# Down projection of a decoder layer: the residual put into three PSUM banks by ScalarE, four merged sums, and the last gated chunk turned, fetched and split at other places in the order

## The chip, the core and the metric

The kernel runs on one core of one Trainium2 chip. The metric is the device time of one execution in microseconds (us); lower is better. TensorE (PE, with its weight loads PEld), VectorE (DVE), ScalarE (ACT), GpSimd (POOL) and SyncE (SP, which here only issues DMAs) each run their own list of instructions in order and wait for each other by semaphores.

## The reference, cut to what matters

One decoder layer over 256 tokens of width 1024, all in float32: a mixer, a cross-attention, and a SwiGLU feed-forward block, each followed by a residual sum and a layer norm. The change is in the last block:

```
h2  = layer_norm(ALPHA * h1 + cross_attention, ln2)          # 256 x 1024
g   = silu(h2 @ w_gate) * (h2 @ w_up)                        # 256 x 2816
out = layer_norm(ALPHA * h2 + g @ w_down, ln3)               # 256 x 1024
```

ALPHA is the fourth root of 2. The last line is what the changed code computes: the product with `w_down`, the residual `ALPHA * h2`, and the sum of the two.

## The kernel before, in words

**Products.** Every float32 operand is split into a high and a low part that TensorE can multiply exactly enough: ScalarE rounds the operand to `hi`, VectorE subtracts it (`lo = x - hi`), and each product is three matmuls (hi by hi, lo by hi, hi by lo; function `three`, L351 to L353). Weight rows come from HBM by SP's DMAs into raw buffers (`w133r`), and the splits of one weight row are one ScalarE copy (`w133h`, L144 or L157) and one VectorE subtraction (`w133l`, L145 or L158), both 128x1024. There are nine buffers for split weights and seven for raw ones.

**Gate and up.** The 2816 columns are eleven chunks of 256 (`NFC = 11`, c = 0 to 10). For each chunk, `proj_n` makes two PSUM banks `pg` (one per 128 tokens, t = 0 and 1), then `gated(c, t, ...)` takes the silu on ScalarE (L942) and the product on VectorE (L943) into `sg`.

**Turning a chunk.** For the down product, g must lie with its columns on the partitions. `gated_out(c)` transposes `sg` in 32x32 blocks on VectorE (`gs<-sg`, L435) and sends it to DRAM by one DMA on SP's queue (`gd<-gs`, L438). `gated_in(c)` reads it back by four DMAs on SP's queue (`gr<-gd`, L446). `gated_split(c)` splits it: `gTh` on ScalarE (L414), `gTl` on VectorE (L415).

**Down.** The output of 256x1024 is four quadrants: C11, C12 (tokens 0 to 127, left and right half), C21, C22 (tokens 128 to 255), each one PSUM bank; in the code they are `acc[PIECES[0]]` to `acc[PIECES[3]]`. For the first nine chunks (`SEVEN = 9`) the products use Strassen's scheme with seven products for eight, where four of them (p1, p5, p6, p7) are gathered in banks of their own (`shared`, made during the gate-and-up loop by `shared_products`), and the others go straight into C11, C12 and C21. The merge is C11 += p1, C12 += p1+p6+p5, C21 += p1+p6+p7, C22 += p1+p6+p7+p5. The last two chunks (four weight rows, w135 to w138) are multiplied in the plain way, quadrant after quadrant, in the tail of `down()`; C22 is made there in two pieces of 256 columns, the second in a bank of its own (`own`).

**The order around the change.** All engines run in the order in which the code issues. `down()` is a generator that yields after each product; a loop of 23 steps (step 0 to 22) runs it, and a table `events` says what is issued ahead of which step. One product is 3 matmuls. Steps 0 to 22 cover all products of the first nine chunks except four that go into C21 later; behind step 22 come the seeds (below) and the plain products of C11, C12, C21 and the two pieces of C22. The function `get` also issues the splits of weight rows, nine rows ahead, so these lie between the events on ScalarE and VectorE.

**Merge and residual before.** `merge()` runs in eight parts at steps 8, 9, 11, 13, 14, 16, 17 and 19: it copies p1 to SBUF on ScalarE (`u1`, L1103), and makes on VectorE, in eight instructions of 128x512, the sums u2 and u3 and, for each quadrant, `r = ALPHA * h2 + sum` (L1100, and L1110, L1119 for p5). The four `r` are then added to the banks ("seeds", L1068): for C12 and C21 behind step 22, for C22's two pieces behind C11's statistics, and for C11 in the sum L1174. C22's bank gets its first two matmuls (L1157) ahead of C21's products, so that there is something to add to.

**The end.** Per 128 tokens: statistics (`bn_stats`, L715, two to four of them), their aggregate (L722), a power on POOL (L724), and two passes on VectorE per half (L729 or L1182, then L735), then the stores. The last piece of tokens 128 to 255 ends on TensorE and ScalarE (L1209 to L1217).

Of the kernel before, what the change touches and what calls it, by code (L numbers as in the profile page):

```python
# [11 lines left out]
OP = mybir.AluOpType  # L12
AX = mybir.AxisListType

P = 128
D = 1024
S = 256
T = S // P
# [6 lines left out]
NFC = DFF // CW  # L25
WINDOWS = (2, 4, 8, 16)
PADW = 16
ALPHA = 2.0 ** 0.25
# [7 lines left out]
SEVEN, LAG, LATE = 9, 2, 4  # L36
# [6 lines left out]
class Stream:  # L43
# [118 lines left out]
    def next(self):  # L162

        i = len(self.tiles)
        return i + (2 if i < len(self.items) and self.items[i][0] == "sums" else 1)
# [6 lines left out]
    def get(self, numbers, k):  # L172

        n = self.count(numbers[0])
        self.prepare(numbers[k // n] + 1, True)
        self.asked += 1
        if not self.held and self.asked % self.pace == 0:
            self.prepare(min(self.used + AHEAD, self.next()))
        hi, lo = self.tiles[numbers[k // n]]
        return hi[:, k % n, :], lo[:, k % n, :]  # L180
# [13 lines left out]
def decoder_layer(  # L194
# [3 lines left out]
    nc = tc.nc  # L198
# [17 lines left out]
    def accbank(name):  # L216
        return pa.tile([P, 512], F32, tag="acc", name=name)


    ws = Stream(nc, wp)  # L220
# [42 lines left out]
    for c in range(NFC):  # L263
        c_gu.append(ws.add(w_gu[c], 4))
        n = c - LAG
# [89 lines left out]
    def pair(hl, *ix):  # L355
        return hl[0][ix], hl[1][ix]

    ALL = slice(None)
# [46 lines left out]
    def run(gen, n=None):  # L405

        while n is None or n > 0:
            if next(gen, gen) is gen:
                return False
            n = None if n is None else n - 1  # L410
        return True

    def split(h, l, ps):
        nc.scalar.copy(h, ps)  # L414
        nc.vector.tensor_sub(l, ps, r32(h))  # L415
# [227 lines left out]
    v, u, xk = do_v(), do_u(), do_xk()  # L643
# [102 lines left out]
    PIECES = tuple((t, *half) for t in range(T) for half in HALVES)  # L746
# [49 lines left out]
    for t in range(T):  # L796
        norm = Norm(1, xt[:, t, :], h1[:, t, :])
# [105 lines left out]
    h2 = ap.tile([P, T, D], F32, tag="a8", name="h2")  # L903
# [17 lines left out]
    norm = Norm(2, h1[:, 0, :], h2[:, 0, :])  # L921
# [3 lines left out]
    norm = Norm(2, h1[:, 1, :], h2[:, 1, :])  # L925
# [13 lines left out]
    def gated(c, t, ps):  # L939

        sg = sgs[c][:, :, t, :]
        nc.scalar.activation(sg, ps[:, :CW].rearrange("p (f b) -> p f b", f=2), AF.Silu, bias=0.0, scale=1.0)  # L942
        nc.vector.tensor_mul(sg, sg, ps[:, CW:].rearrange("p (f b) -> p f b", f=2))  # L943
# [3 lines left out]
    def gated_out(c):  # L947
        via[c] = turned([(0, sgs[c].rearrange("p f t b -> p (f t) b"))], 4, "g")

    def gated_in(c):  # L950
        via[c] = landed(via[c], 4, "g")
# [25 lines left out]
    def fourth_split(c0, c1):  # L977
        hl = [sp.tile([P, 4, P], F32R, name=f"S4{n}", tag="pr", bufs=PR_BUFS) for n in range(2)]
        for c in range(c0, c1):
            s4[c] = hl[0][:, c - c0], hl[1][:, c - c0]  # L980
        split(*[s[:, :c1 - c0] for s in hl], s_raw["fourth"][:, c0:c1])

    def gated_split(c):
        i, f = divmod(2 * c, KD)
        h, l = [g[:, f:f + 2, :].rearrange("p f (t i b) -> p (f t) i b", t=T, i=4) for g in gT[i]]
        split(h, l, via[c].rearrange("p i m b -> p m i b"))

    begun = set()
# [37 lines left out]
    def by_row():  # L1026

        for gen in gu1:
            while run(gen, 2):
                yield  # L1030

    for c in range(1, NFC):
        sgs.append(sp.tile([P, 2, T, P], F32, name="sg", tag="pr", bufs=PR_BUFS))
        pss = {t: second[t] if c == 1 else accbank("pg") for t in range(T)}
        gu = by_row() if c == 1 else proj_n(pss, c_gu[c], h2T)
        run(gu, 1)
        gated_out(c - 1)
        run(gu, 2)
        if c > 1:
            gated_split(c - 2)  # L1040
            if c - 2 < SEVEN:
                token_sums(c - 2)
        run(gu, 2)
        gated_in(c - 1)
        run(gu, 1)
        if 0 <= c - 2 < SEVEN:
            token_sums_split(c - 2)
        if c == NFC - 1:
            fourth_split(0, 4)
        run(gu)  # L1050
        for t in range(T):
            gated(c, t, pss[t])
        if 0 <= c - LAG < SEVEN:
            shared_products(c - LAG)

# [3 lines left out]

    LAST = 768  # L1060
    norms = []
    acc = {PIECES[n]: accbank("acc") for n in (2, 0, 1, 3)}
    C11, C12, C21, C22 = [acc[piece] for piece in PIECES]
    acc[1, 512, LAST] = C22[:, :LAST - 512]

    def seed(t, c0, c1, ps):

        nc.vector.tensor_add(ps, norms[t].r[:, c0:c1], ps)  # L1068

    def four(c0, c1):  # L1070

# [16 lines left out]
    def merge():  # L1088

        p1, p5, p6, p7 = shared  # L1090
        for t in range(T):
            norms.append(Norm(3, h2[:, t, :]))
        r = [norms[t].r[:, h * 512:(h + 1) * 512] for t in range(T) for h in range(2)]
        tok = [h2[:, t, h * 512:(h + 1) * 512] for t in range(T) for h in range(2)]

        def u(i):
            return sp.tile([P, 512], F32, name=f"u{i}", tag="pr", bufs=PR_BUFS)

        def onto(n, u):
            nc.vector.scalar_tensor_tensor(r[n], tok[n], ALPHA, u, op0=OP.mult, op1=OP.add)  # L1100

        u1, u2 = u(1), u(2)
        nc.scalar.copy(u1, p1)  # L1103
        nc.vector.tensor_add(u2, u1, p6)
        yield
        onto(0, u1)
        yield
        onto(1, u2)
        yield
        nc.vector.tensor_add(r[1], r[1], p5)  # L1110
        yield
        u3 = u(3)
        nc.vector.tensor_add(u3, u2, p7)
        yield
        onto(2, u3)
        yield
        onto(3, u3)
        yield
        nc.vector.tensor_add(r[3], r[3], p5)  # L1119
        yield  # L1120

    def down():

        yield from fourth(SEVEN - 1, SEVEN)
        yield from four(SEVEN - 1, SEVEN)
        for c in range(0, SEVEN - 1, 2):
            if c < LATE:
                yield from fourth(c, c + 2)
            yield from four(c, c + 2)
        load_norm("g", 3, ln3_g)()  # L1130
        load_norm("b", 3, ln3_b)()
        get = lambda k: (gT[k // KD][0][:, k % KD], gT[k // KD][1][:, k % KD])
        rest = [c_dn[c][f] for c in range(SEVEN, NFC) for f in range(2)]
        done = 2 * SEVEN
        acc[1, LAST, D] = bank("acc")[:, :D - LAST]
        ws.prepare(ws.used + AHEAD)
        ws.held = True
        seed(*PIECES[1], acc[PIECES[1]])
        seed(*PIECES[2], acc[PIECES[2]])
        for piece in (*PIECES[:3], (1, 512, LAST), (1, LAST, D)):  # L1140
            t, c0, c1 = piece
            if piece == PIECES[2]:
                for c in range(LATE, SEVEN - 1, 2):
                    yield from fourth(c, c + 2)
            for j, numbers in enumerate(rest):
                y_hi, y_lo = pair(get(done + j), ALL, slice(t * P, (t + 1) * P))
                hi, lo = [w[:, c0:c1] for w in ws.get(numbers, 0)]
                end = j == len(rest) - 1
                if j or (t, c0) not in ((1, 512), (1, LAST)):
                    nc.tensor.matmul(acc[piece], y_hi, hi, start=False, stop=False, skip_group_check=True)  # L1150
                nc.tensor.matmul(acc[piece], y_hi, lo, start=False, stop=False, skip_group_check=True)
                nc.tensor.matmul(acc[piece], y_lo, hi, start=False, stop=end, skip_group_check=True)
                yield
            if piece == PIECES[1]:
                y_hi = pair(get(done), ALL, slice(P, 2 * P))[0]
                for c0, c1 in ((512, LAST), (LAST, D)):
                    nc.tensor.matmul(acc[1, c0, c1], y_hi, ws.get(rest[0], 0)[0][:, c0:c1], start=True, stop=False,  # L1157
                                     skip_group_check=True)
            yield piece

    dn, parts = down(), merge()
    events = {
        2: lambda: gated_out(NFC - 1), 4: lambda: fourth_split(4, SEVEN - 1), 6: lambda: gated_split(NFC - 2),
        7: lambda: gated_in(NFC - 1), 18: lambda: gated_split(NFC - 1),
    }
    events.update({step: lambda: run(parts, 1) for step in (8, 9, 11, 13, 14, 16, 17, 19)})
    for step in range(23):
        events.get(step, lambda: None)()
        run(dn, 1)
# [1 line left out]
    until(dn)  # L1171
    norm = norms[0]
    for c in (0, 256):
        nc.vector.tensor_add(norm.r[:, c:c + 256], norm.r[:, c:c + 256], acc[PIECES[0]][:, c:c + 256])  # L1174
        norm.measure(c, c + 256)

    def measure(norm, ps):
        for c in range(0, ps.shape[1], 256):
# [5 lines left out]

    until(dn)
    own = acc[1, LAST, D]
    seed(1, 512, LAST, acc[1, 512, LAST])
    seed(1, LAST, D, own)
    measure(norm, acc[PIECES[1]])
    norm.stats()  # L1190
    norm.centre(0, 512)
# [8 lines left out]
    norm = norms[1]  # L1200
# [67 lines left out]
```

## Time and profile before

| | |
|---|---|
| median of 3 runs | 371.18 us (371.0 to 372.96) |
| the profiled execution | 370.71 us; its span from first to last instruction 368.9 us |
| TensorE busy | 360.5 us, 98% of the span, 1995 matmuls |
| VectorE busy | 312.1 us, 85% |
| ScalarE busy | 197.3 us, 53% |
| POOL busy | 68.9 us, 19% |
| granted TensorE clock | 0.996 |
| HBM traffic | 241 GB/s over the span |

The profile is of one execution. All times on the timeline are microseconds from the span's start. A row of the timeline is: start, duration, engine, line, operation, output<-inputs, shape, count, and in brackets how long the engine had been idle and what released it. The duration of an instruction is longer than its distance to the next one where two overlap in the engine's pipeline: TensorE's 128x512 matmuls have 0.39 us each and start 0.23 us apart. The line numbers L are those of the kernel before, unless the text says otherwise.

### The profile page before, as it was taken

What the parts mean: (1) busy time and instruction counts of PE and PEld (TensorE: products, weight loads), DVE (VectorE), ACT (ScalarE), POOL (GpSimd) and SP (SyncE); (2) the same over time, 40 slices, a digit from 0 to 9 for tenths busy, and PEclk for the clock granted to TensorE, in tenths of its full rate; (3) what the DMA queues carried; (4) which work ended last, traced back from release to release, by engine and by line L of the source; (5) the groups of instructions that cost most, each with busy time, mean ns of one, the idle gap of its engine ahead of it and who ended that gap; (6) DMA issues with size and microseconds to landing.
All of it is one profiled execution on the core that took longest, in us unless ns stands there. A gap on an engine that the chain in (4) does not pass through costs nothing.

```text
span 368.9 us, 5709 instructions
## 1 busy us (share of the span) xinstructions
PE 360.5 (98%) x1995; PEld 311.3 (84%) x1995; DVE 312.1 (85%) x462; ACT 197.3 (53%) x298; POOL 68.9 (19%) x102
## 2 busy tenths in 40 slices
PE   9999999999999999999999999999999999999893
PEld 9997998997888899988888888888888888888682
DVE  5778899994699788765879989999998999789974
ACT  5666865753153665564127636754764664579101
POOL 1000058140010003220010024315402422400000
PEclk9999999999999999999999999999999999999998
DMA  7997699699525995944105988779769877656311
GB/s 246 416 421 297 207 318 327 247 253 396 211 89 167 370 372 203 329 148 151 57 2 198 344 287 285 289 245 346 266 224 338 274 270 262 225 170 195 117 49 65
DMA packets 33836, 89.24 MB, mean 242 GB/s; under 512 B 4240, under 2 KB 12304, under 8 KB 33680
## 3 DMA queue, kind: packets, MB, share of 16 engines
q1 hardware_dynamic: 31520, 83.77, 64.0%
q0 software_dynamic: 1712, 4.72, 4.0%
q10 hardware_dynamic: 576, 0.39, 0.3%
q8 instruction: 15, 0.25, 0.3%
q14 instruction: 13, 0.11, 0.1%
HBM read 81.53 MB, written 7.34 MB: 241 GB/s over the span
## 4 chain that ended last, share of the span: by engine, by line
PE 93%; DVE 4%; issue 1%; ACT 0%; DVEq 0%
PE pg L352 11%; PE pg L351 11%; PE pg L353 11%; PE pxk L369 6%; PE pxq L369 6%; PE pqk L487 6%; PE acc L351 4%; PE acc L352 4%; PE acc L353 4%; PE pu L369 3%; PE x L352 2%; PE x L351 2%; PE x L353 2%; PE xv L352 2%; PE xv L351 2%; PE xv L353 2%
## 5 line engine op out<-in xcount | busy, mean ns | idle before, releaser
L962 POOL TENSOR_TENSOR sraw<-gr 128x128 f32<-128x128 f32 x9 | 9.8, 1094 | 94.7 <-DMA gr<-gd 87.8
L724 POOL TENSOR_TENSOR rs<-mv,mhalf 128x1 f32<-128x1 f32 x6 | 4.4, 735 | 100.2 <-DVE mv L722 100.2
L438 POOL DMA_DIRECT2D pd<-ps x4 | 2.4, 612 | 48.4 <-DVE ps L435 48.1
L524 ACT ACTIVATE pr<-pr,mx 128x128 f32<-128x128 f32 (+1 forms) x16 | 7.1, 444 | 8.2 <-DVE mx L555 8.2
L963 POOL TENSOR_TENSOR sraw<-sraw,gr 128x128 f32<-128x128 f32 x9 | 10.7, 1192 | 0.7
L1204 ACT COPY r<-acc 128x512 f32<-128x512 f32 (+1 forms) x2 | 1.0, 480 | 17.2 <-DVE st L715 17.1
L414 ACT CAST h2Th<-tp 128x512 fp32r<-128x512 f32 x4 | 2.4, 588 | 14.6 <-PE tp L425 14.6
L446 POOL DMA_DIRECT2D pt<-pd x16 | 8.8, 555 | 6.6 <-ACT w23h L144 3.7
L942 ACT ACTIVATE sg<-pg 128x256 f32<-128x256 f32 x22 | 7.9, 381 | 3.2 <-PE pg L353 3.1
L964 POOL TENSOR_TENSOR sraw<-gr 128x128 f32<-128x128 f32 x9 | 9.1, 1009 | 0.0
L943 DVE TENSOR_TENSOR sg<-sg,pg 128x256 f32<-128x256 f32 x22 | 8.4, 415 | 0.4 <-ACT sg L942 0.3
L446 POOL DMA_DIRECT2D xr<-xd x12 | 6.6, 560 | 8.5 <-DMA xd<-xs 5.3
L414 ACT CAST gTh<-gr 128x512 fp32r<-128x512 f32 x11 | 6.8, 614 | 2.6 <-DMA gr<-gd 2.6
L415 DVE TENSOR_TENSOR gTl<-gr,gTh 128x512 fp32r<-128x512 f32 x11 | 7.8, 708 | 0.4 <-ACT gTh L414 0.4
L438 POOL DMA_DIRECT2D xd<-xs x3 | 1.7, 576 | 34.0 <-DVE xs L435 34.0
L435 DVE STREAM_TRANSPOSE gs<-sg 128x512 f32<-128x512 f32 x11 | 7.7, 701 | 0.0
L729 DVE SCALAR_TENSOR_TENSOR r<-r,mv,g 128x512 f32<-128x512 f32 (+1 forms) x10 | 7.5, 781 | 0.2
L524 ACT ACTIVATE xpr<-xs,mx 128x256 f32<-128x256 f32 x8 | 3.7, 470 | 7.0 <-DVE mx L535 7.0
L414 ACT CAST S<-sraw 128x384 fp32r<-128x384 f32 (+1 forms) x9 | 4.7, 523 | 4.6 <-POOL sraw L964 4.6
L715 DVE BATCH_NORM_STATS2 st<-r 128x6 f32<-128x512 f32 (+1 forms) x10 | 6.4, 641 | 0.3
L529 DVE RECIPROCAL sm<-sm 128x2 f32<-128x2 f32 x12 | 2.0, 164 | 5.5 <-ACT xpr L524 4.4
L531 DVE TENSOR_SCALAR pr<-pr,sm 128x128 f32<-128x128 f32 (+1 forms) x16 | 6.1, 422 | 0.3
(1389 smaller groups left out, 1501.0 us busy)
## 6 DMA issues: line engine op xcount, KB each, us to landing
gd<-gs SPq DMA_DIRECT2D x11, 256.0 KB, 5.5
gr<-gd SPq DMA_DIRECT2D x44, 64.0 KB, 2.0
pd<-ps POOLq DMA_DIRECT2D x4, 384.0 KB, 4.2
pt<-pd POOLq DMA_DIRECT2D x16, 96.0 KB, 7.3
g<-in_ln_g SPq DMA_DIRECT2D x3, 512.0 KB, 4.4
b<-in_ln_b SPq DMA_DIRECT2D x3, 512.0 KB, 6.1
wr<-in_w_qkv SPq DMA_DIRECT2D x5, 256.0 KB, 4.8
mr<-in_mem_t SPq DMA_DIRECT2D x1, 1024.0 KB, 12.0
```

The lines of the kernel that those rows point to most:

```text
L351: nc.tensor.matmul(ps, wa, ya, start=start, stop=False, skip_group_check=part)
L352: nc.tensor.matmul(ps, wa, yb, start=False, stop=False, skip_group_check=part)
L353: nc.tensor.matmul(ps, wb, ya, start=False, stop=stop, skip_group_check=part)
L369: nc.tensor.matmul(pss[f], w[:, s], y, start=k == 0 and f == 0 and n == 0, stop=k == KD - 1 and n == 2, skip_group_check=True)
L414: nc.scalar.copy(h, ps)
L446: queue.dma_start(raw[32 * j:32 * (j + 1)].rearrange("p i m b -> p i (m b)"), via[:, j, :].rearrange("(i a) r -> a i r", i=4))
L487: nc.tensor.matmul(qk[i][:, f, :], w[:, c * P:(c + 1) * P], y, start=k == 0 and f == 0 and w is hi and y is x_hi, stop=k == KD - 1 and w i ...
L524: nc.scalar.activation(dst[:, j, :], src[:, j, :], AF.Exp, bias=mx[:, j:j + 1], scale=sign, accum_out=sm[:, j:j + 1])
L943: nc.vector.tensor_mul(sg, sg, ps[:, CW:].rearrange("p (f b) -> p f b", f=2))
L962: nc.gpsimd.tensor_add(s1, a21, a22)
L963: nc.gpsimd.tensor_sub(s2, s1, a11)
L964: nc.gpsimd.tensor_sub(s3, a11, a21)
```

## The change

It does five things.

1. The residual goes into PSUM first. A new function `residual(n)` takes quadrant n's bank and writes `ALPHA * h2` into it by one ScalarE instruction (128x512). It is called for C21 and C11 in the last round of the gate-and-up loop, ahead of that round's remaining products, and for C12 behind `gated` of the last chunk. The banks are noted as begun, so that the products add to what is there.
2. `merge()` makes four sums without the residual (p1; p1+p6+p5; p1+p6+p7; that + p5) in one ScalarE copy and four VectorE adds, of which the first makes p1+p6 for the other three: at steps 8, 16 and 17, and the last one (C22's) behind C11's sum and statistics.
3. The seeds of C12 and C21 add `merged[n]`; C11's sum reads `merged[0]`; C22's two pieces are now written by VectorE (`ALPHA * h2 + merged[3]`, L1182 of the changed kernel) ahead of all their products.
4. C22's two early matmuls go back to the head of their own pieces, so all products there add.
5. The last chunk: `gated_out(10)` moves from step 2 to directly behind `gated` of that chunk, `gated_in(10)` from step 7 to step 5, `gated_split(10)` from step 18 to step 12.

```diff
+    acc = {}
+
+    def residual(n):
+
+        t, c0, c1 = PIECES[n]
+        acc[PIECES[n]] = accbank("acc")
+        begun.add(id(acc[PIECES[n]]))
+        nc.scalar.mul(acc[PIECES[n]], h2[:, t, c0:c1], ALPHA)
...
             fourth_split(0, 4)
+            residual(2)
+            residual(0)
         run(gu)
         for t in range(T):
             gated(c, t, pss[t])
+        if c == NFC - 1:
+            gated_out(c)
+            residual(1)
         if 0 <= c - LAG < SEVEN:
             shared_products(c - LAG)
...
-    acc = {PIECES[n]: accbank("acc") for n in (2, 0, 1, 3)}
+    acc[PIECES[3]] = accbank("acc")
+    merged = {}
...
-        u1, u2 = u(1), u(2)
-        nc.scalar.copy(u1, p1)
-        nc.vector.tensor_add(u2, u1, p6)
+        merged.update({n: u(n) for n in (0, 4)})
+        nc.scalar.copy(merged[0], p1)
+        nc.vector.tensor_add(merged[4], merged[0], p6)
         yield
-        onto(0, u1)
+        merged[1] = u(1)
+        nc.vector.tensor_add(merged[1], merged[4], p5)
         yield
-        onto(1, u2)
+        merged[2] = u(2)
+        nc.vector.tensor_add(merged[2], merged[4], p7)
         yield
-        nc.vector.tensor_add(r[1], r[1], p5)
-        yield
-        u3 = u(3)
-        nc.vector.tensor_add(u3, u2, p7)
-        yield
-        onto(2, u3)
-        yield
-        onto(3, u3)
-        yield
-        nc.vector.tensor_add(r[3], r[3], p5)
-        yield
+        merged[3] = u(3)
+        nc.vector.tensor_add(merged[3], merged[2], p5)
...
-        seed(*PIECES[1], acc[PIECES[1]])
-        seed(*PIECES[2], acc[PIECES[2]])
+        for n in (1, 2):
+            nc.vector.tensor_add(acc[PIECES[n]], merged[n], acc[PIECES[n]])
...
-            if piece == PIECES[1]:
-                y_hi = pair(get(done), ALL, slice(P, 2 * P))[0]
-                for c0, c1 in ((512, LAST), (LAST, D)):
-                    nc.tensor.matmul(acc[1, c0, c1], y_hi, ws.get(rest[0], 0)[0][:, c0:c1], start=True, stop=False,
-                                     skip_group_check=True)
...
-        2: lambda: gated_out(NFC - 1), 4: lambda: fourth_split(4, SEVEN - 1), 6: lambda: gated_split(NFC - 2),
-        7: lambda: gated_in(NFC - 1), 18: lambda: gated_split(NFC - 1),
+        4: lambda: fourth_split(4, SEVEN - 1), 5: lambda: gated_in(NFC - 1), 6: lambda: gated_split(NFC - 2),
+        12: lambda: gated_split(NFC - 1),
     }
-    events.update({step: lambda: run(parts, 1) for step in (8, 9, 11, 13, 14, 16, 17, 19)})
+    events.update({step: lambda: run(parts, 1) for step in (8, 16, 17)})
...
-        nc.vector.tensor_add(norm.r[:, c:c + 256], norm.r[:, c:c + 256], acc[PIECES[0]][:, c:c + 256])
+        nc.vector.tensor_add(norm.r[:, c:c + 256], merged[0][:, c:c + 256], acc[PIECES[0]][:, c:c + 256])
         norm.measure(c, c + 256)
+    run(parts)
...
-    seed(1, 512, LAST, acc[1, 512, LAST])
-    seed(1, LAST, D, own)
+    for c0, c1 in ((512, LAST), (LAST, D)):
+        nc.vector.scalar_tensor_tensor(acc[1, c0, c1], h2[:, 1, c0:c1], ALPHA, merged[3][:, c0 - 512:c1 - 512],
+                                       op0=OP.mult, op1=OP.add)
```

The first place is VectorE in the second half of the 23 steps, from the split of w134 to the seeds of C12 and C21. `u` are the merged sums, `x` the banks of p5 to p7, `h` is h2, `r` the residual sums, `gTl` is here the last chunk's low part. Before:

```order
L158 TENSOR_TENSOR w134l<-t_3106,w134h 128x1024
L1100 SCALAR_TENSOR_TENSOR r<-h_1881,u_3604 128x512
L145 TENSOR_TENSOR w135l<-w130r,w135h 128x1024
L1110 TENSOR_TENSOR r<-r,x 128x512
L145 TENSOR_TENSOR w136l<-w131r,w136h 128x1024
L1113 TENSOR_TENSOR u_3640<-u_3604,x 128x512
L145 TENSOR_TENSOR w137l<-w132r,w137h 128x1024
L1100 SCALAR_TENSOR_TENSOR r<-h_1881,u_3640 128x512 x2
L145 TENSOR_TENSOR w138l<-w133r,w138h 128x1024
L415 TENSOR_TENSOR gTl_2066<-gr,gTh_2065 128x512
L1119 TENSOR_TENSOR r<-r,x 128x512
L1068 TENSOR_TENSOR acc<-r,acc 128x512 x2
```

And the same stretch of VectorE's list after the change (with the changed kernel's line numbers):

```order
L158 TENSOR_TENSOR w134l<-t_3106,w134h 128x1024
L145 TENSOR_TENSOR w135l<-w130r,w135h 128x1024
L415 TENSOR_TENSOR gTl_2066<-gr,gTh_2065 128x512
L145 TENSOR_TENSOR w136l<-w131r,w136h 128x1024
L145 TENSOR_TENSOR w137l<-w132r,w137h 128x1024
L1113 TENSOR_TENSOR u_3652<-u_3607,x 128x512
L1116 TENSOR_TENSOR u_3657<-u_3607,x 128x512
L145 TENSOR_TENSOR w138l<-w133r,w138h 128x1024
L1138 TENSOR_TENSOR acc<-u_3652,acc 128x512
L1138 TENSOR_TENSOR acc<-u_3657,acc 128x512
```

The last chunk's `gTl` moved from behind w138l to ahead of w136l, and between w134l and the seeds six instructions of 128x512 became two.

The second place is ScalarE in the last round of the gate-and-up loop, as one piece of the difference: `acc` at L1039 of the changed kernel is the new write of the residual, `w126h` and `w127h` are weight rows, `sg` the silu of the last chunk.

```order
 L414 CAST S_3486<-S_2413 128x512
+L1039 ACTIVATE acc<-h_1881 128x512 x2
 L157 CAST w126h<-t_2588 128x1024
 L942 ACTIVATE sg<-pg 128x2x128 x2
+L1039 ACTIVATE acc<-h_1881 128x512
 L144 CAST w127h<-w124r 128x1024
 L144 CAST w128h<-w125r 128x1024
```

Two writes stand ahead of w126h and one between the silu and w127h; nothing was taken away there.

The third place is SP's list of DMAs around the last chunk's way through DRAM (`gd` out, `gr` back):

```order
 L122 DMA w130r<-in_w_down 128x1024
 L446 DMA gr<-gd 32x4x128 x4
+L438 DMA gd<-gs 128x512
 L122 DMA w131r<-in_w_down 128x1024
 L122 DMA w132r<-in_w_down 128x1024
 L122 DMA w133r<-in_w_down 128x1024
-L438 DMA gd<-gs 128x512
 L446 DMA gr<-gd 32x4x128 x4
```

The way out now stands ahead of the last three weight rows; the way back stays behind them.

More of the change, by code (lines that the diff above doesn't have):

```diff
@@ L1061, in decoder_layer @@
     norms = []
-    acc = {PIECES[n]: accbank("acc") for n in (2, 0, 1, 3)}
+    acc[PIECES[3]] = accbank("acc")
+    merged = {}
     C11, C12, C21, C22 = [acc[piece] for piece in PIECES]
     acc[1, 512, LAST] = C22[:, :LAST - 512]
-    def seed(t, c0, c1, ps):
-        nc.vector.tensor_add(ps, norms[t].r[:, c0:c1], ps)
     def four(c0, c1):
@@ L1092, in merge @@
             norms.append(Norm(3, h2[:, t, :]))
-        r = [norms[t].r[:, h * 512:(h + 1) * 512] for t in range(T) for h in range(2)]
-        tok = [h2[:, t, h * 512:(h + 1) * 512] for t in range(T) for h in range(2)]
         def u(i):
             return sp.tile([P, 512], F32, name=f"u{i}", tag="pr", bufs=PR_BUFS)
-        def onto(n, u):
-            nc.vector.scalar_tensor_tensor(r[n], tok[n], ALPHA, u, op0=OP.mult, op1=OP.add)
-        u1, u2 = u(1), u(2)
-        nc.scalar.copy(u1, p1)
-        nc.vector.tensor_add(u2, u1, p6)
+        merged.update({n: u(n) for n in (0, 4)})
+        nc.scalar.copy(merged[0], p1)
+        nc.vector.tensor_add(merged[4], merged[0], p6)
         yield
-        onto(0, u1)
+        merged[1] = u(1)
+        nc.vector.tensor_add(merged[1], merged[4], p5)
         yield
-        onto(1, u2)
+        merged[2] = u(2)
+        nc.vector.tensor_add(merged[2], merged[4], p7)
         yield
-        nc.vector.tensor_add(r[1], r[1], p5)
-        yield
-        u3 = u(3)
-        nc.vector.tensor_add(u3, u2, p7)
-        yield
-        onto(2, u3)
-        yield
-        onto(3, u3)
-        yield
-        nc.vector.tensor_add(r[3], r[3], p5)
-        yield
+        merged[3] = u(3)
+        nc.vector.tensor_add(merged[3], merged[2], p5)
     def down():
@@ L1148, in down @@
                 end = j == len(rest) - 1
-                if j or (t, c0) not in ((1, 512), (1, LAST)):
-                    nc.tensor.matmul(acc[piece], y_hi, hi, start=False, stop=False, skip_group_check=True)
+                nc.tensor.matmul(acc[piece], y_hi, hi, start=False, stop=False, skip_group_check=True)
                 nc.tensor.matmul(acc[piece], y_hi, lo, start=False, stop=False, skip_group_check=True)
```

## The prediction, made before the result was known

> **What bounds the kernel now.** I read the page's busy times first, then what TensorE waited for, then the engines in the last windows of the down product, and last the timelines of TensorE, VectorE, ScalarE and SP there. The page:
>
> ```profile
> PE 360.5 (98%) x1995; PEld 311.3 (84%) x1995; DVE 312.1 (85%) x462; ACT 197.3 (53%) x298; POOL 68.9 (19%) x102
> ```
>
> TensorE is busy all but 8.4 us of the span, and the change takes no matmul away. So it can win only where TensorE stands still. Its waits (engine, line waited for, us in total, times, longest) name two places in the part that the change touches:
>
> ```profile
> PE acc L1152 <- DVE gTl L415: 1.8, 1, 1.8
> PE out L1213 <- ACT diag L1211: 1.5, 1, 1.5
> ```
>
> The second is in the last layer norm, behind all that is changed. The first is the last chunk's low part, `gTl`. The windows around it (PE, PEld, DVE, ACT, POOL busy, clock, DMA share, GB/s):
>
> ```profile
> 335.00:340.00 5.00, 5.00 (x24) 4.13 (x23) 5.00 (x8) 4.70 (x6) 0.00 (x0) 1.00 0.47 174
> 340.00:345.00 5.00, 5.00 (x24) 4.14 (x23) 5.00 (x7) 2.75 (x4) 0.00 (x0) 1.00 0.71 205
> 345.00:350.00 5.00, 3.23 (x15) 2.37 (x14) 5.00 (x8) 0.00 (x0) 0.00 (x0) 1.00 0.11 44
> ```
>
> VectorE has no free moment there, while ScalarE has run out of work: VectorE's list is late, and TensorE catches up with it. The loss, from TensorE's timeline:
>
> ```profile
> 345.66 0.39 PE L1150 MATMUL acc<-w135h,gTh 128*128 128x512 f32 x1
> 347.25 0.39 PE L1151 MATMUL acc<-w137l,gTh 128*128 128x512 f32 x1
> 349.41 0.50 PE L1152 MATMUL acc<-w137h,gTl 128*128 128x512 f32 x1 [1.77 <-DVE gTl L415]
> 350.21 0.39 PE L1152 MATMUL acc<-w138h,gTl 128*128 128x512 f32 x1
> 350.61 0.50 PE L1150 MATMUL acc<-w135h,gTh 128*128 128x512 f32 x1
> 353.48 0.40 PE L1157 MATMUL acc<-w135h,gTh 128*128 128x256 f32 x2
> 361.69 0.28 PE L1152 MATMUL acc<-w138h,gTl 128*128 128x256 f32 x1
> ```
>
> From 345.66 to 347.25 are seven starts, 0.227 us each. From 347.25 to 353.48 are seventeen (the four left of C11's twelve, twelve of C12, and L1157): 3.86 us at that pace, 6.23 in fact. So 2.37 us are lost: 1.93 ahead of 349.41, 0.17 ahead of 350.61 (C12's first product, behind its seed), the rest in slower starts right after each stop.
>
> **The change part by part.** VectorE first, since the gap closes only if its list gets there in time:
>
> ```profile
> 333.59 0.70 DVE L435 STREAM_TRANSPOSE gs<-sg 128x512 f32<-128x512 f32 x1
> 334.22 1.18 DVE L158 TENSOR_TENSOR w131l<-t,w131h 128x1024 fp32r<-128x1024 f32 x1
> 339.39 0.68 DVE L1100 SCALAR_TENSOR_TENSOR r<-h,u 128x512 f32<-128x512 f32 x1
> 339.99 1.22 DVE L158 TENSOR_TENSOR w134l<-t,w134h 128x1024 fp32r<-128x1024 f32 x1
> 341.13 0.68 DVE L1100 SCALAR_TENSOR_TENSOR r<-h,u 128x512 f32<-128x512 f32 x1
> 347.54 1.22 DVE L145 TENSOR_TENSOR w138l<-w133r,w138h 128x1024 fp32r<-128x1024 f32 x1
> 348.67 0.68 DVE L415 TENSOR_TENSOR gTl<-gr,gTh 128x512 fp32r<-128x512 f32 x1
> 349.87 1.28 DVE L1068 TENSOR_TENSOR acc<-r,acc 128x512 f32<-128x512 f32 x2
> ```
>
> By the distance to the next start a 128x512 costs 0.60 us and a 128x1024 1.14. Ahead of `gTl` now go: onto C11, onto C12, C12's p5, u3, and two onto C21 and C22 (six, 3.60), and w136l, w137l, w138l (3.42): 7.02 us. Ahead of the seed of C12 seven of the old merge instructions go (4.20) and two new ones come (1.20).
>
> ScalarE's three new writes act ahead of that:
>
> ```profile
> 323.58 0.61 ACT L414 CAST S<-S 128x512 fp32r<-128x512 f32 x1
> 324.78 1.06 ACT L157 CAST w126h<-t 128x1024 fp32r<-128x1024 f32 x1 [0.59 <-PE pg L353]
> 326.82 0.38 ACT L942 ACTIVATE sg<-pg 128x256 f32<-128x256 f32 x1 [0.98 <-PE pg L353]
> 327.50 0.38 ACT L942 ACTIVATE sg<-pg 128x256 f32<-128x256 f32 x1 [0.30 <-PE pg L353]
> 327.78 1.04 ACT L144 CAST w127h<-w124r 128x1024 fp32r<-128x1024 f32 x1
> 337.70 1.06 ACT L144 CAST w135h<-w130r 128x1024 fp32r<-128x1024 f32 x1
> 342.74 0.61 ACT L414 CAST gTh<-gr 128x512 fp32r<-128x512 f32 x1
> 328.85 1.23 DVE L145 TENSOR_TENSOR w127l<-w124r,w127h 128x1024 fp32r<-128x1024 f32 x1 [0.52 <-ACT w127h L144]
> ```
>
> No row shows ScalarE writing 128x512 from SBUF into PSUM. The bounds are the silu of half the width (0.38) and the copy of twice the width (1.06); the nearest is the 128x512 cast, 0.61 us or, by its distance to a next start, 0.52, which I take. Two writes from 324.10 end at 325.1: w126h is 0.4 late, and the 0.98 us of idle time ahead of the silu swallow that. The third must wait until VectorE has read the bank, about 327.9, and makes w127h end near 329.45 in place of 328.82. Behind it in ScalarE's line stand w127h to w135h, for which VectorE waits. VectorE fills the wait with `gs` (0.63 by its distance to the next), which it no longer does at 333.59: w127l starts at 329.47, and w131l, four times 1.14 later, at 334.03 in place of 334.22. So VectorE's list is 0.19 early when the merge begins. TensorE's first product into C12's bank, 21 products of 3 x 0.227 ahead of 345.66, starts at 331.4; the third write ends at 328.5.
>
> Then `gTl` starts at 348.67 - 7.02 - 0.19 = 341.46; w138l, ahead of which 6 x 0.60 went and `gTl` and two sums came, at 347.54 - 0.19 - 1.80 = 345.55, done by 346.8; the seed of C12 at 349.87 - 0.19 - 4.20 + 1.20 = 346.68, done by 347.4. TensorE, running on at 0.227 from 345.66, needs `gTl` for the ninth start, 347.48, w138l at 347.93, and the seed of C12 at 348.38. All three are there, w138l and the seed about 1.0 us early: these are what is late next.
>
> The way through DRAM: can `gTh` be cast in time?
>
> ```profile
> 334.32 0.33 SPq L438 DMA_DIRECT2D gd<-gs  x1
> 338.61 1.75 SPq L446 DMA_DIRECT2D gr<-gd  x4
> 332.56 0.33 SPq L122 DMA_DIRECT2D w133r<-in_w_down  x1
> DMA to landing us min/median/max: 1.8/2.0/4.1
> ```
>
> The last row is for `gr`'s 44 issues. Before, the way out took 338.61 - 334.32 = 4.29. Now `gs` ends at about 329.0, `gd` leaves at 329.05 and is there at 333.35; w133r, which stands ahead of `gr`, leaves when w129l is read, about 332.9, so it costs nothing; four issues and a landing of 2.0 give 337.1. ScalarE comes to the cast behind w135h, at 337.70 + 1.06 = 338.76. Its 0.52 there delays w136h to w138h, of which VectorE wants the first at 342.1; before, ScalarE was through with all of them at 342.74. The three weight rows that `gd` passed leave up to 0.6 us later and are first needed by w136h, which now stands behind the cast. The loads of the last norm's g and b only go out earlier, behind `gr`. By the Trainium skill's "DMA: Bandwidth & Descriptors" (Latency and other measured facts) HBM answers in 0.2 us on average and in 2 us under high load; the old way out ran at a DMA share of about 0.47, the new one goes among weight rows. An estimate by that page adds 1.8 to each leg and brings the data at 340.7, the cast at 341.3; the sum stays, and the cover is nearly used up.
>
> The rest of the path. C22's pieces begin at 348.38 + 36 x 0.227 = 356.55, the two L1157 matmuls only change place. VectorE's tail:
>
> ```profile
> 353.80 0.76 DVE L1068 TENSOR_TENSOR acc<-r,acc 128x256 f32<-128x256 f32 x2 [0.88 <-PE acc L1157]
> 359.38 0.43 DVE L715 BATCH_NORM_STATS2 st<-acc 128x6 f32<-128x256 f32 x1 [0.94 <-PE acc L1152]
> ```
>
> C11's part took about 1.8 us before 353.80 - 0.88 and now starts at 348.5, when its last matmul ends; then come C22's last sum (0.60) and its two writes (0.76, as the adds), to 351.7, 4.8 us ahead of TensorE's need. The other half's norm (358.44 - 354.56 = 3.9) ends at 355.6, ahead of C21's statistics near 356.7. So it waits there as now, and the end follows TensorE.
>
> The sum: -2.37 us on TensorE, nothing added: span 366.5, profiled execution 370.71 - 2.37 = 368.3. The median lies 0.47 above the profiled execution; from it, 371.18 - 2.37 = **368.8 us** (-0.64%).
>
> **The rivals.**
>
> *VectorE is still a little late.* Its margin is 1.0 us. A ScalarE write of price p moves the seed's end to 346.85 + p and w138l's to 346.25 + p, so from p = 1.5 up TensorE stops again, and at p = 3.9 the gain is gone. The bounds 0.38 to 1.06 speak against it; that no row shows this write, and that VectorE would have to keep its 0.60 and 1.14 without a hole for 20 us, speak for it. Half of the gain lost: 370.0. The Trainium skill's "ScalarE: Activation LUTs" (Rules for kernel authors) wants a multiplication on VectorE, up to about 3 times faster per element in bf16. Three times 0.60 would be p = 1.8, with 0.3 us lost, 369.1; the rows here, float32, have 0.68 for VectorE's 128x512 and 0.61 for ScalarE's.
>
> *The hop is late (the other side).* `gTh` now stands in ScalarE's line ahead of w136h to w138h, and `gTl` ahead of the same rows on VectorE; where it waited last, it holds up three weight rows. `gTl` may start at 342.5 without harm; at 344.9 the gain is gone; at 346.8 the kernel is 1.9 us slower, 373.1. That needs a landing near 346, 17 us after `gd` leaves, in place of 8. Over all DMAs that write or read `gd`:
>
> ```profile
> DMA to landing us min/median/max: 1.8/2.0/6.6
> ```
>
> The longest of these for the way out and the longest `gr` give 329.05 + 6.6 + 1.75 + 4.1 = 341.5, and `gTl` near 342.1: still no loss. It would take delays that this trace has nowhere.
>
> *The pause is closed and the end does not follow.* If VectorE's norm of tokens 0 to 127 were late by more than its 1.1 us of slack, it would set the end: up to the whole 2.4 us, 371.2. But C21's statistics need not start the moment that TensorE is done with C21, only in time for the last piece 2.8 us later, so this is unlikely.
>
> **How the numbers follow.** The full gain 0.75, VectorE a little late 0.15, the hop late enough to be slower 0.04, the end not following 0.06. The full gain gives 368.2 (with 0.3 more from starts that are no longer slow, and 0.3 of spread) to 369.2; to hold 8 in 10 the range takes in half the gain lost: 368.2 to 370.1. About 0.5% (1.9 us) is what a measurement can tell from no change. The full gain lies 0.5 us beyond it, so I leave it under the bound once in ten: faster 0.75 x 0.9 + 0.15 x 0.1 = 0.69; slower 0.04; the rest, 0.27, the same.
>
> **What would show it.** Right: no wait of TensorE for `gTl` or a seed between 345 and 357, starts 0.227 apart there; the last C22 matmul near 359.3; `gTl` near 341.5; ScalarE's writes at 0.5 to 0.6. Wrong: TensorE waiting for `w138l` or for L1138 (VectorE late), ScalarE idle ahead of `gTh` for the DMA (hop late), or the last statistics started by VectorE's own list (the end doesn't follow).

## The result, and the profile after the change

| | before | after |
|---|---|---|
| median of 6 runs each, taken side by side | 371.42 us | 369.40 us |
| ratio, with its 95% interval | | 0.994 (0.9918 to 0.9961) |
| profiled execution, its span | 370.71 us, 368.9 us | 369.47 us, 367.7 us |

The kernel became 2.0 us faster. The page of the changed kernel has the same matmuls, 0.4 us less of TensorE's busy time and 2.2 us less of VectorE's:

```profile
PE 360.1 (98%) x1995; PEld 311.3 (85%) x1995; DVE 309.9 (84%) x458; ACT 198.4 (54%) x301; POOL 67.4 (18%) x102
```

TensorE's waits after the change:

```profile
PE out L1208 <- ACT diag L1206: 1.5, 1, 1.5
PE po L591 <- DVE mx L555: 0.8, 1, 0.8
PE busy L458 <- PEq L1227: 0.8, 1, 0.8
PE pqk L487 <- ACT w3h L144: 0.2, 1, 0.2
```

The wait for `gTl` is gone and no seed has taken its place. Two waits are new, for `po` and `pqk`; both lie in the first 65 us, in code that the change does not touch. Two of the windows, of which the second is the one in which TensorE stood still before:

```profile
335.00:340.00 5.00, 5.00 (x24) 4.14 (x23) 5.00 (x7) 4.87 (x6) 0.00 (x0) 1.00 0.98 338
345.00:350.00 5.00, 5.00 (x24) 4.14 (x23) 4.36 (x7) 0.00 (x0) 0.00 (x0) 1.00 0.00 0
```

From 345 to 350 TensorE works 5.00 of 5.00 (3.23 before) and VectorE, which was busy for all of that window before, has 0.64 us to spare. TensorE's timeline:

```profile
346.79 0.39 PE L1148 MATMUL acc<-w135h,gTh 128*128 128x512 f32 x1
348.60 0.39 PE L1150 MATMUL acc<-w137h,gTl 128*128 128x512 f32 x1
349.51 0.39 PE L1148 MATMUL acc<-w135h,gTh 128*128 128x512 f32 x1
360.42 0.28 PE L1150 MATMUL acc<-w138h,gTl 128*128 128x256 f32 x1
```

A measure that does not depend on when the stage starts is the stretch from the first plain matmul (w135, C11) to the last one of C22: 360.42 - 346.79 = 13.63 us, against 361.69 - 345.66 = 16.03 before. That is 2.40 us. But the stretch begins at 346.79 in place of 345.66, so only 1.2 us of it are seen in these two spans.

VectorE, and then ScalarE (the rows of the new writes, of what stands behind them, and of the last chunk):

```profile
342.57 0.68 DVE L415 TENSOR_TENSOR gTl<-gr,gTh 128x512 fp32r<-128x512 f32 x1
346.64 1.22 DVE L145 TENSOR_TENSOR w138l<-w133r,w138h 128x1024 fp32r<-128x1024 f32 x1
347.78 1.28 DVE L1138 TENSOR_TENSOR acc<-u,acc 128x512 f32<-128x512 f32 x2
357.87 0.43 DVE L715 BATCH_NORM_STATS2 st<-acc 128x6 f32<-128x256 f32 x1 [1.02 <-PE acc L1150]
```

```profile
325.23 1.11 ACT L1039 ACTIVATE acc<-h 128x512 f32<-128x512 f32 x2
326.28 1.03 ACT L157 CAST w126h<-t 128x1024 fp32r<-128x1024 f32 x1
327.95 0.38 ACT L942 ACTIVATE sg<-pg 128x256 f32<-128x256 f32 x1 [0.63 <-PE pg L353]
328.93 0.60 ACT L1039 ACTIVATE acc<-h 128x512 f32<-128x512 f32 x1
329.47 1.04 ACT L144 CAST w127h<-w124r 128x1024 fp32r<-128x1024 f32 x1
341.12 0.62 ACT L414 CAST gTh<-gr 128x512 fp32r<-128x512 f32 x1 [1.23 <-DMA gr<-gd]
```

Counted from the first plain matmul, `gTl` starts at -4.22 us (before: +3.01), w138l at -0.15 (+1.88), the seed of C12 at +0.99 (+4.21). ScalarE still idles ahead of the silu, so the two early writes cost nothing. In the last layer norm VectorE waits for TensorE as before (1.02 us ahead of C21's statistics), and from the start of the last C22 matmul to the end of the span it is 7.3 us (7.2 before). The one thing that came otherwise is the last row: ScalarE stands 1.23 us for the chunk's way back. SP's timeline, and the landings of the last chunk's four reads (`gr` from 333.5 to 345):

```profile
330.24 0.34 SPq L438 DMA_DIRECT2D gd<-gs  x1
334.06 0.33 SPq L122 DMA_DIRECT2D w133r<-in_w_down  x1
334.50 2.08 SPq L446 DMA_DIRECT2D gr<-gd  x4
```

```profile
DMA to landing us min/median/max: 4.9/5.6/5.8
```

The four reads are issued where they were expected, but land in 4.9 to 5.8 us, in a window in which the DMA engines are 0.98 busy. In the kernel before, the same four (issued at 338.61, 6.05 us behind w133r in place of 0.44) landed in:

```profile
DMA to landing us min/median/max: 1.8/1.9/2.0
```

### The profile page after: what moved, and what is told of

Its sections match the earlier page's. It is cut to its first block, busy times and chain, and to the rows that moved or that the text cites. A ratio compares the mean times of both kernels' runs of the same rounds, so it can differ in the third digit from the quotient of the medians.

```text
span 367.7 us, 5709 instructions
## 1 busy us (share of the span) xinstructions
PE 360.1 (98%) x1995; PEld 311.3 (85%) x1995; DVE 309.9 (84%) x458; ACT 198.4 (54%) x301; POOL 67.4 (18%) x102
## 4 chain that ended last, share of the span: by engine, by line
PE 90%; DMA 4%; DVE 2%; POOL 1%; issue 1%; SPq 1%; ACT 0%; DVEq 0%; POOLq 0%; ACTq 0%
PE pg L353 11%; PE pg L351 11%; PE pg L352 11%; PE pxq L369 6%; PE acc L351 6%; PE acc L352 6%; PE acc L353 6%; PE pqk L487 5%; PE pxk L369 5%; DMA pd<-ps 2%; PE x L353 2%; PE x L351 2%; PE x L352 2%; PE xv L353 2%; PE xv L352 2%; PE xv L351 2%
## 5 line engine op out<-in xcount | busy, mean ns | idle before, releaser
L962 POOL TENSOR_TENSOR sraw<-gr 128x128 f32<-128x128 f32 x9 | 7.2, 803 | 95.4 <-DMA gr<-gd 70.0
L964 POOL TENSOR_TENSOR sraw<-gr 128x128 f32<-128x128 f32 x9 | 9.5, 1057 | 0.0
L967 POOL TENSOR_TENSOR S<-gr,sraw 128x128 f32<-128x128 f32 x8 | 6.6, 829 | 0.0
```

The source lines that it names most:

```text
L964: nc.gpsimd.tensor_sub(s3, a11, a21)
```

## The experiments

Two theories stood against each other. Mine: VectorE's list ahead of C12's seed is what TensorE waited for, and the gain comes from making that list shorter (the residual written early, four sums in place of eight instructions). The rivals: the gain is that of the chunk turned and split sooner, or that of ScalarE taking work over. The stretch from the first plain matmul to the last decides best, since it leaves out what happens earlier; it is given for each run beside the time, which is compared with the kernel before on the same chip. The median of the kernel before is 371.39 us beside the chunk alone, the residual with the sums, the residual by VectorE and the three more sums. It is 371.81 us beside the residual by VectorE with the old way, the four more writes, the g load and the repeat of the changed kernel.

The stretches came nearer to their forecasts than the times. By the medians the gain was 0.25 to 0.56 us smaller than the forecast's range for the residual with the sums (1.95 us), the three more sums (0.84) and the four more writes (0.69), 0.2 smaller than forecast for the chunk alone (0.53), and 0.45 larger than the range in the repeat of the changed kernel (2.85). The other two came within 0.1 us of theirs.

### The chunk's way moved, nothing else

```diff
+        if c == NFC - 1:
+            gated_out(c)
...
-        2: lambda: gated_out(NFC - 1), 4: lambda: fourth_split(4, SEVEN - 1), 6: lambda: gated_split(NFC - 2),
-        7: lambda: gated_in(NFC - 1), 18: lambda: gated_split(NFC - 1),
+        4: lambda: fourth_split(4, SEVEN - 1), 5: lambda: gated_in(NFC - 1), 6: lambda: gated_split(NFC - 2),
+        12: lambda: gated_split(NFC - 1),
```

> The kernel before, with only the last chunk's way moved (out behind its silu and product, back at step 5, split at step 12); the residual and the merge as before. My theory, VectorE's length of list ahead of the seeds: the eight merge instructions and the seeds stand where they stood, so w138l is done 3.0 us after TensorE's first plain matmul (L1150, w135) and needed at 2.27, and C12's seed is done at 4.2 and needed at 2.72: TensorE loses about 1.7 of the 2.4 us still, waiting for w138l and the seed in place of gTl; the stretch from that first plain matmul to the last one of C22 takes 15.3 us (16.0 before, 13.6 after the change). Time 0.7 us below before. Rival, that the gain is the earlier chunk's: no wait for gTl, stretch 13.6 to 13.8, time 2.2 to 2.4 us below before.

Measured: 370.86 us, ratio 0.9978 (0.9962 to 0.9994); stretch 15.43 us. TensorE's waits:

```profile
PE acc L1153 <- DVE w138l L145: 0.7, 1, 0.7
PE acc L1152 <- DVE acc L1070: 0.5, 1, 0.5
```

The wait for `gTl` is gone, and the next two things on VectorE's list are late in its place: w138l and the seed of C12. Moving the chunk alone brings 0.6 of the 2.4 us (the forecast was a loss of 1.7 left over; it is 15.43 - 13.63 = 1.80).

### The residual and the sums, with the chunk's way as before

The edit to the changed kernel puts the three steps of the last chunk back to 2, 7 and 18:

```diff
-            gated_out(c)
...
-        4: lambda: fourth_split(4, SEVEN - 1), 5: lambda: gated_in(NFC - 1), 6: lambda: gated_split(NFC - 2),
-        12: lambda: gated_split(NFC - 1),
+        2: lambda: gated_out(NFC - 1), 4: lambda: fourth_split(4, SEVEN - 1), 6: lambda: gated_split(NFC - 2),
+        7: lambda: gated_in(NFC - 1), 18: lambda: gated_split(NFC - 1),
```

> The changed kernel with the last chunk's way where it was (out at step 2, back at step 7, split at step 18). My theory: VectorE is through with w138l at 1.1 us, with gTl at 1.74 (needed at 1.82) and with C12's seed at 2.34 (needed at 2.72) behind TensorE's first plain matmul, so all but 0.1 us of the gain stays: stretch 13.6 to 13.8 us, time 2.2 to 2.4 us below before. Rival, that the gain is the earlier chunk's: TensorE still waits 1.0 to 1.9 us for gTl, stretch 14.6 to 15.5 us, time 0.5 to 1.4 us below before.

Measured: 369.44 us, ratio 0.994 (0.9926 to 0.9955); stretch 13.70 us, no wait of TensorE in it. VectorE's timeline; TensorE's first plain matmul was at 347.03:

```profile
346.87 1.22 DVE L145 TENSOR_TENSOR w138l<-w133r,w138h 128x1024 fp32r<-128x1024 f32 x1
348.01 0.68 DVE L415 TENSOR_TENSOR gTl<-gr,gTh 128x512 fp32r<-128x512 f32 x1
348.61 1.28 DVE L1137 TENSOR_TENSOR acc<-u,acc 128x512 f32<-128x512 f32 x2
```

`gTl` stands behind w138l again and is done 1.66 us after the first plain matmul, 0.16 before it is needed. The shorter list brings the gain; the earlier chunk brings room.

### The residual written by VectorE

```diff
-        nc.scalar.mul(acc[PIECES[n]], h2[:, t, c0:c1], ALPHA)
+        nc.vector.tensor_scalar(acc[PIECES[n]], h2[:, t, c0:c1], ALPHA, None, op0=OP.mult)
```

> The changed kernel with the three residual writes made by VectorE at the same places. My theory, that it is the place that counts and not the engine: VectorE stands idle there for about 1 us in all before its list fills up, and takes three more instructions of 0.3 to 0.6 us; w127l starts within 0.2 us of where it does in the changed kernel, stretch from the first plain matmul to the last 13.6 us, time 2.2 to 2.4 us below before. Rival, that ScalarE's taking over is what pays: VectorE's list gets 1.8 us longer up to the seed, TensorE loses 0.8 us, stretch 14.4 us or more, time 1.5 us below before.

Measured: 368.95 us, ratio 0.9931 (0.9915 to 0.9946); stretch 13.63 us, no wait. VectorE's timeline, with TensorE's first plain matmul at 346.47:

```profile
326.34 1.28 DVE L1039 TENSOR_SCALAR acc<-h 128x512 f32<-128x512 f32 x2
330.08 0.67 DVE L1039 TENSOR_SCALAR acc<-h 128x512 f32<-128x512 f32 x1
330.65 1.20 DVE L145 TENSOR_TENSOR w127l<-w124r,w127h 128x1024 fp32r<-128x1024 f32 x1
347.86 1.29 DVE L1138 TENSOR_TENSOR acc<-u,acc 128x512 f32<-128x512 f32 x2
```

Counted from the first plain matmul, w127l starts at -15.82 us, 0.43 later than in the changed kernel (330.54 - 346.79 = -16.25); the forecast was within 0.2. So of the three writes' 1.8 us VectorE makes about 1.4 in time in which it had stood idle, and the other 0.4 come out of its margin: C12's seed starts at +1.39 in place of +0.99 and is still in time. That ScalarE makes them is not what pays.

### The residual by VectorE and the chunk's way as before

Both of the last two edits together, no others.

> The changed kernel with the three residual writes on VectorE and with the last chunk's way where it was before the change: what is left is the residual's early place and the four sums. My theory, that this alone is the gain: VectorE starts w127l about 16.4 us ahead of the first plain matmul, is done with gTl about 1.5 us behind it (needed at 1.82) and with C12's seed at 2.1 (needed at 2.72); stretch 13.6 to 13.75 us, time 1.9 to 2.4 us below before. Rival, that either ScalarE's help or the early chunk is needed: TensorE waits 0.3 us or more for gTl or the seed, stretch 14.0 us or more.

Measured: 369.33 us, ratio 0.9922 (0.9899 to 0.9944); stretch 13.63 us. VectorE's timeline, with TensorE's first plain matmul at 346.89:

```profile
326.76 1.28 DVE L1039 TENSOR_SCALAR acc<-h 128x512 f32<-128x512 f32 x2
329.75 0.68 DVE L1039 TENSOR_SCALAR acc<-h 128x512 f32<-128x512 f32 x1
347.56 0.68 DVE L415 TENSOR_TENSOR gTl<-gr,gTh 128x512 fp32r<-128x512 f32 x1
348.16 1.28 DVE L1137 TENSOR_TENSOR acc<-u,acc 128x512 f32<-128x512 f32 x2
```

With neither ScalarE's help nor the earlier chunk, `gTl` is done at +1.35 and C12's seed at about +1.95, needed at +1.82 and +2.72. The early residual and the four sums, with what belongs to them (C22's pieces written late, its two early matmuls moved back), are the whole of the gain. These parts were not run apart, so how the gain divides among them is not shown.

### Three more sums on VectorE

```diff
-        nc.vector.tensor_add(merged[2], merged[4], p7)
+        for _ in range(4):
+            nc.vector.tensor_add(merged[2], merged[4], p7)
```

> The changed kernel with the sum of C21 made four times over (the same result each time), that is three more VectorE instructions of 128x512, 1.8 us, ahead of w138l and the seeds. My theory, a margin of 1.0 us on VectorE: TensorE waits 0.6 us for w138l and 0.15 for C12's seed, with slow starts 0.8 to 1.0 in all; stretch 14.4 to 14.6 us, time 1.4 to 1.6 us below before. Rival, that VectorE was never that close (the wait for gTl alone was the loss): no wait, stretch 13.6 us, time as the changed kernel, 2.2 to 2.4 below before.

Measured: 370.55 us, ratio 0.9982 (0.9963 to 1.0); stretch 14.96 us. VectorE's row of the four sums, and TensorE's wait:

```profile
345.47 2.85 DVE L1117 TENSOR_TENSOR u<-u,x 128x512 f32<-128x512 f32 x4
```

```profile
PE acc L1150 <- DVE w138l L145: 0.9, 1, 0.9
```

The size was missed, since the three take 2.17 us in place of 1.8: each writes the tile that the one before it writes, and starts 0.72 later. Of these 2.17 us, 1.18 reach C12's first product (it starts at 350.11, where 346.21 + 12 x 0.227 = 348.93 would have been in time). So the margin was 2.17 - 1.18 = 0.99, as the prediction had it (1.0); the rest of the 14.96 - 13.63 = 1.33 us are slower starts behind the stop.

### Four more writes on ScalarE

```diff
-        nc.scalar.mul(acc[PIECES[n]], h2[:, t, c0:c1], ALPHA)
+        for _ in range(5 if n == 1 else 1):
+            nc.scalar.mul(acc[PIECES[n]], h2[:, t, c0:c1], ALPHA)
```

> The changed kernel with ScalarE's third write of the residual (C12) made five times over, the same values each time: 4 x 0.54 = 2.2 us more on ScalarE ahead of w127h. My theory, the prediction's formula (TensorE stops again from a price of 1.5 us up): VectorE, which waits for w127h, runs its whole list 2.2 us later; TensorE waits about 0.9 us for w138l and 0.2 for C12's seed, stretch 14.7 to 15.0 us, time 1.0 to 1.3 us below before. Rival, that ScalarE has room for it (it idles 1.2 us later on, waiting for the chunk, and is done 4 us ahead of VectorE): no wait, stretch 13.63 us, time 1.9 to 2.4 us below before.

Measured: 371.12 us, ratio 0.997 (0.9952 to 0.9988); stretch 15.30 us. ScalarE's timeline, and TensorE's wait:

```profile
329.11 3.14 ACT L1040 ACTIVATE acc<-h 128x512 f32<-128x512 f32 x5
332.18 1.03 ACT L144 CAST w127h<-w124r 128x1024 fp32r<-128x1024 f32 x1
```

```profile
PE acc L1150 <- DVE w138l L145: 1.2, 1, 1.2
```

The five take 332.18 - 329.11 = 3.07 us in place of 0.54, 2.53 more where 2.2 was forecast. The prediction's formula (TensorE stops from 1.5 us up) gives 3.07 - 1.5 = 1.57 us of loss; measured are 15.30 - 13.63 = 1.67. So the third write is on the path to VectorE's list, with room for about one more microsecond; ScalarE's idle time later does not help. The run raises the price of the third write alone; the first two stand where ScalarE idles 0.63 us ahead of the silu, and what a higher price of theirs would do was not run.

### The g load behind the b load

```diff
-        load_norm("g", 3, ln3_g)()
         load_norm("b", 3, ln3_b)()
+        load_norm("g", 3, ln3_g)()
```

> The changed kernel with the loads of the last norm's g and b in the other order: b must wait for VectorE's w134l, so no 512 KB load goes out right behind the four reads of the last chunk. One look at the chunk's landing. Theory, that g's load delays the reads: ScalarE's wait for the chunk (1.2 us in the changed kernel, 1.0 in the kernel with three more sums) falls below 0.4. Rival, that the weight rows w131 to w133 ahead of them do: it stays at 0.8 to 1.2. The stretch stays at 13.63 by both.

Measured, one run: 368.57 us, stretch 13.63 us. ScalarE's wait for the chunk:

```profile
339.62 0.62 ACT L414 CAST gTh<-gr 128x512 fp32r<-128x512 f32 x1 [0.61 <-DMA gr<-gd]
```

0.61 us lies between what the two theories wanted. It is below the six other traces with the reads at this place (1.0 to 1.7; 1.01 in the repeat below), but the reads still land in 4.5 to 5.4 us, where the other six have 4.8 to 6.0. The load of g may be a smaller part of what delays the reads and the weight rows ahead of them the larger; one run doesn't settle it. It costs no time: VectorE comes to `gTl` later than that in all these runs.

### Both kernels again: where the stretch starts

Nothing is edited: the changed kernel and, twice, the kernel before.

> The changed kernel once more, beside the next two on the same chip. My theory: stretch from the first plain matmul (L1148, w135) to the last one of C22 13.63 us again, since no wait lies in it; where it starts differs by up to 1.4 us from run to run (by the first weight loads and the chunks' ways through DRAM long before the change), so the total lies 1.9 to 2.4 us below before. Rival, that the changed kernel itself runs later ahead of the stretch than the kernel before: the start of the stretch stays at 346.8 or later and the total is no more than 1.5 us below before.

> The kernel before, profiled once more. My theory: its first profiled execution was an early one, and ahead of the changed code both kernels run alike; the stretch from the first plain matmul (L1150, w135) to the last one of C22 takes 16.0 us again, and it starts between 345.9 and 347.0, where the changed kernel and its variants start it. Rival, that the change makes the kernel later ahead of the stretch: it starts within 0.1 us of 345.66 again.

> The kernel before, profiled a third time, for the same question. Theory: stretch 16.0 us, starting between 345.9 and 347.0. Rival: it starts within 0.1 us of 345.66 again.

Measured: the changed kernel 368.96 us, ratio 0.9909 (0.9883 to 0.9935), stretch 13.64 us from 346.71; the kernel before 371.17 and 371.51 us (one run each), stretches 16.00 and 16.05 us from 346.15 and 346.44. In both of these TensorE has a wait at 157 us that its first profile did not have:

```profile
PE xs L353 <- DVE xq L419: 0.5, 1, 0.5
```

The stretch is the same to 0.05 us each time; its start is not. The kernel before has it at 345.66, 346.15 and 346.44, the changed kernel at 346.79 and 346.71, and with only g and b swapped at 345.92. The differences arise where the two lists are still the same: in the first weight loads (w1 to w3, up to 1 us), at `po` near 63 us and at `xs` near 157. From the first matmul with w55 (172.94 us in the kernel before, 174.05 in the changed one) to the first plain matmul all twelve traces take 172.7 us, alike to 0.1. So what differs has happened before 175 us, 150 us ahead of the first changed instruction. The profile on which the prediction rests was an early execution, and that of the changed kernel a late one. All the same, the eight traces with the residual early start the stretch 0.5 us later on average (345.92 to 347.03) than the four without (345.66 to 346.44); whether that is chance is not shown.

## Why the prediction came out as it did

- *TensorE's loss of 2.37 us, all of it to be won.* Right: 2.40 by the stretches, and 2.0 and 2.85 by the medians of two comparisons. The first one's interval (1.4 to 3.0 us) holds it; the second's (2.42 to 4.35) begins just above it.
- *VectorE's list.* Right to a few hundredths: from the first plain matmul, `gTl` was forecast at -4.20, w138l at -0.11, the seed at +1.02, and found at -4.22, -0.15 and +0.99. Adding up start distances from the old trace, in the new order, was enough.
- *ScalarE's writes.* Taken at 0.52 each; they take 0.60, or 0.51 to 0.54 to the next start. w126h was 0.37 late (0.4 forecast), and the silu's idle time swallowed it.
- *VectorE's margin of 1.0 us, and the price p from which it is gone.* Shown by the two kernels with more on VectorE and on ScalarE, which lost about what the margin and the formula leave; for p this holds of the third write, the only one made longer.
- *The hop.* This step failed in its parts, though not in what it was to show. The reads were issued 4.26 us behind `gd`, forecast 4.30, but that is luck: the forecast took the old way out of 4.29, while `gd` landed in 2.0 us, and it was w133r, said to cost nothing, behind which SP issued them (334.06, then 334.50). "A landing of 2.0" failed: the four reads landed in 4.9 to 5.8 us. The 2.0 was the median of 44 old reads, of which the last four went out 6 us behind the last weight row. The cast began 1.23 us later than ScalarE was ready for it, which the prediction had named as a sign of being wrong, but it was done 0.8 us before VectorE came to it, so TensorE lost nothing. The estimate by the Trainium skill's "DMA: Bandwidth & Descriptors" (Latency and other measured facts), 3.8 us for the way back, is nearer than 2.0 but below the 4.9 to 5.8 measured; its 1.8 us more on the way out did not come: `gd` took 2.0 us (4.2 before).

```profile
gd<-gs SPq DMA_DIRECT2D x1, 256.0 KB, 2.0
```

- *The multiplication on ScalarE.* The Trainium skill's "ScalarE: Activation LUTs" (Rules for kernel authors) wants it on VectorE. In float32 the two cost nearly the same (0.60 and 0.68 us), and either engine gives the whole gain, because ScalarE idled there and VectorE for most of what it took.
- *The total.* Forecast 368.8, measured 369.4: the gap is 0.6 us, of which 0.25 is the median of the kernel before (371.42 in the comparison, 371.18 when the forecast was made), and the rest is within what the start of the stretch varies by (1.4 us over the traces). The forecast's span of 366.5 was missed by 1.2 us (367.7): it was made from an execution whose first 345 us were the quickest of those seen.
- *What the working left open.* It added up the moved chunk and the shorter list as one path. The experiments separate them: the list alone is enough, the chunk alone brings a quarter.

No variant beats the changed kernel by more than the comparisons can tell: from the first plain matmul to the last one TensorE has no gap left for this stage to give back.

## What to carry to other kernels

Where a full engine waits for one instruction of another engine's list, removing that wait brings only the distance to the next late item of the same list: write down the deadlines of all of them (here `gTl`, w138l, the seed) before choosing what to move. Work that needs no late input (here a residual) belongs where its engine stands idle earlier; which of two engines makes it matters less than that. Compare traces over a stretch that begins at the changed code, because the time at which the stage starts can differ from run to run by as much as the change is worth.

## What the runs showed of the hardware

- A VectorE or ScalarE instruction repeated onto the place that the one before it writes starts only when that one has ended: 0.72 us later for a VectorE sum of 128x512 of 0.68 us (0.60 with different places), about 0.64 later for a ScalarE write into PSUM of 0.60 us (0.51 for two different banks). The repeated ones also read the same inputs; that it is the common place that counts was not tried apart.
- A ScalarE write of 128x512 float32 from SBUF into PSUM takes 0.60 us, the VectorE one 0.68.
- The last chunk's four reads of 64 KB landed in 4.5 to 6.0 us where they went out 0.4 to 1.6 us behind a 512 KB weight row (seven traces), and in 1.8 to 2.5 us where the last weight row had left 5.4 to 6.3 us earlier (five traces). The 256 KB write landed in 2.0 us ahead of the last three weight rows (the seven) and in 3.6 to 4.5 us behind them (the five).
- The kernels in which TensorE stops in this stage spread more from run to run: the kernel before by 3.4 us (23 runs), with more sums 3.2 (12), with more writes 1.9 (12), with the chunk alone 1.4 (11); those without a stop by 0.5 to 1.3 (5 or 6 runs each). The counts differ. A part of it is the granted TensorE clock of the whole execution: of the 40 runs of the kernel before beside the experiments, seven had 0.991 or 0.992 and took 373.1 to 374.0 us; the other 33 had 0.995 to 0.998 and took 370.6 to 372.3, but for one of 373.3. No run of a kernel without a stop had less than 0.995. What lowers the clock in some runs, no run here tells.
